# Gates of the weight sums through a table of their own, the sums spread over the stages, POOL left to their transfers

## The chip, the cores and the metric

One core of one Trainium2 chip runs the whole program in one launch. The metric is the device time of that launch in microseconds. Five engines are spoken of: PE (TensorE, the matmuls; PEld its weight loads), DVE (VectorE), ACT (ScalarE), POOL (GpSimd) and SP (SyncE, which here only issues transfers). POOL and SP both issue DMAs, POOL through the software queue, SP through the hardware queue.

## What is computed

A trunk of two layers on x of 1024 tokens and 1024 channels, with 256 memory tokens, all in float32. Cut to what matters:

```python
def reference(x, mem, ...):
    m = rms_norm(mem, mem_norm_g)
    h = x
    for layer in range(DEPTH):                      # DEPTH = 2
        hn = rms_norm(h, mix_norm_g[layer])
        if layer % 2 == 0:
            h = h + fourier_na_mixer(hn, w_in_ab[0], rpb[0], w_out_ab[0])
        else:
            h = h + short_gated_conv_mixer(hn, w_in_c[0], conv_c[0], w_out_c[0])
        h = h + memory_cross_attention(rms_norm(h, xa_norm_g[layer]), m, xa_wq[layer], xa_wkv[layer], xa_wo[layer])
        h = h + conv_ffn(rms_norm(h, ffn_norm_g[layer]), ffn_w_up[layer], ffn_conv_w[layer], ffn_conv_b[layer], ffn_w_down[layer])
    return rms_norm(h, final_norm_g)
```

The first mixer projects the 1024 channels to 2048: four Fourier groups of 128 channels (a 2-D FFT, real part) and q, k and v of four neighbourhood attention heads, whose scores get a bias `rpb` inside a window; both halves go through `w_out_ab`. The FFN has 2 x 2048 channels up, a width-3 convolution and a gelu gate, and 2048 back down.

## The kernel before

Every matmul is done as three passes over a number split in a high and a low part (`mm3`, L223 to L227: high x high at L225, high x low at L226, low x high at L227). A split (L218 to L221) is a cast on ACT (L220) for the high part and a subtraction (L221), on DVE or, where the caller says so, on POOL, for the low part. SBUF is a pool of 52 buffers of 128x1024 floats and four halves, all shown as `p`; a buffer is handed on as soon as its last reader is done, so an instruction that writes into it waits for that reader.

The stages follow one another: keys and values of the memory beside the first norm (to about 165 us), mixer 0 (to about 500), cross attention 0 (to about 725), a trunk of up0, down d0, convolution c and its output oc (to about 1515), cross attention 1 (to about 1775), and up1 with down d1 to the end. Inside a stage several generators run side by side (`run`, each with a cost as weight), and a scheduler fixes the order on each engine from them at build time.

Mixer 0 (L824 on) computes 16 blocks of the input projection (`proj_thread`): blocks 0 to 3 for the Fourier groups, 4 to 15 for q, k, v. `fft_thread` (memsets on POOL at L582, L583 and L640) and `na_thread` run beside it. `na_prep` loads for each head the mask (L750) and the bias (L752) by SP and subtracts one from the other on POOL (L753); the scores (L679, on DVE) add the table to what PE left in PSUM. `ahead` splits the four Fourier results, the odd ones on POOL. Then xT is loaded again (L499) and w_out is applied.

The FFNs, the convolution and oc are done by a scheme with seven products in place of eight for 2x2 blocks (Strassen and Winograd). Its weights come in 34 units (up0 8, d0 4, convolution 8, oc 2, up1 8, d1 4). Of each unit products 1, 2 and 4 read a quadrant of the weight, products 7, 6, 3 and 5 a sum of quadrants. These sums are made in DRAM by POOL's queue (`sums`, L1049 to L1063): four gates (L1059), each a DMA of one element from the tile that the caller has just written into the sum's own tile, which hold the copies back until the caller has got there; four copies of a quadrant (L1061); and four DMAs that add another one (L1063). Callers are the posts of the projection (L564, blocks 4 to 15), of the query projection (L883) and of the residual add (L816). `w_load` (L1066) reads a sum by SP when its product is near. `xb1` (L1115 on) starts an FFN: the norm's sum (matmul L328), the operands of the products, with ACT and DVE splits, up to the first result at DVE L1241. `put` (L1204) writes operands of the down projection to DRAM, `plan_down` (L1387) loads them back.

Of the kernel before, what the change touches and what calls it, by code (L numbers as in the profile page):

```python
# [47 lines left out]

CHAIN = {1: "a", 2: "a", 6: "b", 7: "b", 4: "b", 5: "c", 3: "c"}
OPENS, ENDS = (1, 6, 5), (2, 4, 3)  # L50
QUARTERS = ("11", "12", "21", "22")
COUPLES = (((0, 4), (1, 5)), ((2, 6), (3, 7)))


# [74 lines left out]
class Kern:  # L129
    def __init__(self, ctx, tc, ap):  # L130
        self.tc, self.nc, self.ap = tc, tc.nc, ap
        nc = self.nc
        sb = ctx.enter_context(tc.tile_pool(name="sb", bufs=1))
        ps = ctx.enter_context(tc.tile_pool(name="ps", bufs=1, space=bass.MemoryType.PSUM))
        dr = ctx.enter_context(tc.tile_pool(name="dr", bufs=1, space=bass.MemoryType.DRAM))
        self.sb = sb
        self.PSUM = ps.tile([P, 8 * 512], F32, name="PS")
        Pool.tick = 0
        self.pools = {2: Pool(NSLOT), 1: Pool(NHALF)}
        self.banks = Pool(8)  # L140
        self.kvd = [dr.tile([4, P, 2 * U], F32, name=f"kvd{i}") for i in range(2)]
        self.vec = sb.tile([P, NVEC], F32, name="vec")
        nc.sync.dma_start(self.vec, ap["vecs"])

        nc.vector.tensor_scalar(self.vec[:, 0:CONV_C], self.vec[:, 0:CONV_C], -1.0, None, op0=ALU.mult)
        self.ones = sb.tile([P, P], F32, name="ones")
        nc.vector.memset(self.ones, 1.0)
        self.ones_r = sb.tile([P, P], F32R, name="ones_r")
        nc.scalar.copy(self.ones_r, self.ones)
        self.ident = sb.tile([P, P], F32, name="ident")  # L150
        make_identity(nc, self.ident)
        self.eps = sb.tile([P, 1], F32, name="eps")
        nc.vector.memset(self.eps, EPS)
        warm = sb.tile([P, 1], F32, name="warm")
        nc.scalar.activation(warm, self.eps, AF.Abs_reciprocal_sqrt)
        self.small = sb.tile([P, 64], F32, name="small")
        self.nsmall = 0
        self.dr = dr
        self.q, self.did, self.op, self.xd, self.hd, self.wsrc = [], set(), {}, {}, {}, {}
        self.bg = None  # L160


    def sm(self, n):
# [363 lines left out]
    def proj_thread(self, blks, dst, head=0, tail=0, look=LOOK, hooks=()):  # L527

        nc = self.nc

        def psum(b, c):
            if b not in dst:
                dst[b] = [(yield from self.alloc(F32 if b < 4 or b >= 12 else F32R))]
                if 4 <= b < 12:
                    dst[b].append((yield from self.alloc(F32R)))
            self._b = yield from self.bank(1)
            self._bk[(b, c)] = self._b
            return self._b.f()

        self._bk = {}  # L540

        def post(b, c, ps):
            if b < 4:
                nc.scalar.copy(dst[b][0].f(c * CH, (c + 1) * CH), ps)
            else:

                def order(x):
                    return x.rearrange("p (s h r n) -> p s h r n", s=8, h=2, r=8)[:, :, c]
                i = ps.rearrange("p (r s n) -> p s r n", r=8, s=8)
                x = dst[b]  # L550
                if b < 8:
                    t = yield from self.alloc(F32, 1)
                    nc.scalar.activation(t.f(0, CH), ps, AF.Copy, scale=-(float(P) ** -0.5))
                    i = t.f(0, CH).rearrange("p (r s n) -> p s r n", r=8, s=8)
                if b < 12:
                    nc.scalar.copy(order(x[0].r()), i)
                    nc.vector.tensor_tensor(order(x[1].r()), i, order(x[0].f()), op=ALU.subtract)
                    if b < 8:
                        self.free(t)
                else:  # L560
                    nc.scalar.copy(order(x[0].f()), i)
            self.bfree(self._bk.pop((b, c)))
            self.done.add((b, c))
            if b >= 4 and c == 1:  # L564
                self.sums(dst[b][0].f(0, 1)[0:1])

        n = len(blks)
        o = [(blks[b], c) for b, c in self.order(n, min(head, n), tail)]
        yield from self.linear(o, self.ap["w_in"], KT, self.X_hn, psum, post, look=look, hooks=hooks)
# [4 lines left out]
    def fft_thread(self):  # L574
# [4 lines left out]
        nc.sync.dma_start(cs.f(0, 256), self.ap["dft_c"])  # L579
        Cm, Sm = cs.f(0, P), cs.f(P, 2 * P)  # L580
        alt = cs.f(256, 512)
        nc.gpsimd.memset(alt[:, ::2], 1.0)  # L582
        nc.gpsimd.memset(alt[:, 1::2], -1.0)  # L583
        tabs = yield from self.wload(self.ap["dft_s"], 4)
        H = 256

        for g in range(4):
# [49 lines left out]
            eo = yield from self.alloc(F32)  # L637
            y = self.yf[g] = yield from self.alloc(F32)
            nc.vector.scalar_tensor_tensor(e, alt, w[:, 3:4], be.f(0, H), op0=ALU.mult, op1=ALU.add)
            nc.gpsimd.memset(t.f(H, H + 1), 0.0)  # L640
            nc.scalar.copy(t.f(H + 1, 2 * H), bo.f(H + 1, 2 * H))

            nc.vector.scalar_tensor_tensor(y.f(H, H + 1), w[:, 4:5], w[:, 5:6], bo.f(H, H + 1),
# [101 lines left out]
    def na_prep(self, h):  # L745

        nc = self.nc
        hd = {"h": h, "p": {}, "pt": {}}
        m = yield from self.alloc(F32)
        nc.sync.dma_start(m.f(0, 896), self.ap["na_mask"])  # L750
        x = hd["tab"] = yield from self.alloc(F32)
        nc.sync.dma_start(x.f(0, 896), self.ap["na_bias"][h])  # L752
        nc.gpsimd.tensor_tensor(x.f(0, 896), m.f(0, 896), x.f(0, 896), op=ALU.subtract)  # L753
        self.free(m)
        while not self.ready(12 + h):
            yield None
        hd["q"], hd["k"], (x,) = (self.qkv[b + h] for b in (4, 8, 12))
        b = yield from self.bank(2)
        for j in range(8):
            nc.tensor.transpose(b.f(j * P, (j + 1) * P), x.f(j * P, (j + 1) * P), self.ident)  # L760
        hd["v"] = yield from self.wide_split(b.f())
        self.free(x)
        self.bfree(b)
        self.ya[h] = [(yield from self.alloc(F32R)), (yield from self.alloc(F32R))]
        yield 0.9
        return hd
# [34 lines left out]
    def res_post(self, st, fin=None):  # L801
# [8 lines left out]
        def post(b, c, ps):  # L810
# [3 lines left out]
            if st is not None:  # L814
                yield from self.sumsq(st, c, b, hc, CHUNKS[c][1])
                if b % 2 == 1:  # L816
                    self.sums(hc[0:1, 0:1])
            if fin is not None:
                yield from self.gained(fin, c, b)

# [1 line left out]

    def mixer0(self):
        nc = self.nc  # L824
        self.todo = self.up_items(0) + self.down_items("d0", 2, self.ap["w_down"][0])
        self.z, self.yf, self.qkv = {}, {}, {}
        self.done = set()
        self.run((self.proj_thread(range(0, 4), self.z, head=3), 42.0))
# [2 lines left out]
        def ahead():  # L831
            self.free_hn(0)
            for g in range(4):
                y = self.yf[g]
                self.yf[g] = yield from self.wide_split(y.f(), nc.gpsimd if g % 2 else nc.vector)
                self.free(y)

        def main():
# [21 lines left out]
    def xattn(self, l, st):  # L860
# [5 lines left out]
        def qproj(c, hooks=()):  # L866
# [6 lines left out]
            def post(b, cc, ps):  # L873
# [7 lines left out]
                self.bfree(bk.pop(b))  # L881
                qdone[c] = b
                if b % 2 == 1:  # L883
                    self.sums(lo.f(o, o + 1)[0:1])
            yield from self.linear([(b, c) for b in range(KT)], self.ap["wq"][l], KT, self.X_hn, psum, post,
                                   hooks=hooks)
            self.free_hn(c)
# [158 lines left out]
                n -= 1  # L1046


    def sums(self, gate):  # L1049


        if not self.todo:
            return
        key, src, n = self.todo.pop(0)
        g = self.nc.gpsimd
        d = {p: self.dr.tile([P, n], F32, name="ws_%s_%d" % ("_".join(map(str, key)), p)) for p in (7, 6, 3, 5)}
        self.wsrc[key] = {1: src[0], 2: src[1], 4: src[3], **d}
        for p in (7, 6, 3, 5):
            g.dma_start(d[p][0:1, 0:1], gate)  # L1059
        for p, i in ((7, 0), (5, 3), (6, 3), (3, 1)):  # L1060
            g.dma_start(d[p], src[i])  # L1061
        for p, more in ((7, src[2]), (5, src[2]), (6, d[7]), (3, d[6])):
            g.dma_start(d[p], more, accum_op=ALU.add, max_dma_last_dim=1024)  # L1063

    def w_load(self, key, p, n=2):
        def gen():  # L1066
# [134 lines left out]
    def put(self, tag, s, k, p, src):  # L1201

        o = (k % 2) * U
        self.nc.sync.dma_start(self.xd_tile(tag, s, p, k // 2)[:, o:o + U], src)  # L1204

    def put_rest(self, tag, s, k, a, b):

# [12 lines left out]
        self.put(tag, s, k, 5, t1)  # L1220
        self.put(tag, s, k, 3, b22)
        self.free(x, z, a, b)
        self.did.add((tag, "x", s, k))

    def opening(self, q, p, b, u, g, early):

# [160 lines left out]
    def plan_down(self, tag, segs):  # L1387
        def xload(s, p):
            for m in range(2):
                def gen(m=m):  # L1390
                    r = yield from self.alloc(F32)
                    self.nc.sync.dma_start(r.f(), self.xd[tag, s, p, m])
                    self.op.setdefault((tag, "X", s, p), []).append((yield from self.wide_split(r.f())))
                    self.free(r)
                self.task((tag, "X", s, p, m), 3, gen,
                          lambda: all((tag, "x", s, k) in self.did for k in range(4)))

        def row(k):
            def gen():
# [170 lines left out]
    def all(self):  # L1570
# [10 lines left out]
        self.plan_down("d0", 2)  # L1581
        self.plan_conv()
        self.plan_down("oc", 1)
        self.todo += [*self.conv_items(), *self.down_items("oc", 1, self.ap["w_out_c"]), *self.up_items(1)[:4]]
        st = self.xattn(0, st)
        st = self.trunk(st)
        self.plan_up(1)
        self.plan_down("d1", 2)
        self.todo += [*self.up_items(1)[4:], *self.down_items("d1", 2, self.ap["w_down"][1])]
        st = self.xattn(1, st)  # L1590
        self.last(st)

# [34 lines left out]

def _quads(w, pairs):


    return np.stack([np.concatenate([_quad(w, h, pr[e]) for pr in pairs], axis=1)
                     for e in range(2) for h in range(2)])


def _feat(v):
# [91 lines left out]
```

## Time and profile before

| | before |
|---|---|
| median of 3 runs | 2256.32 us (2249.65 to 2257.36) |
| profiled execution | 2262.05 us, span 2260.1, mean granted clock 0.979 |
| PE busy | 2172.6 us (96% of the span) |
| DVE busy | 1457.3 us (64%) |
| ACT busy | 946.1 us (42%) |
| POOL busy | 353.5 us (16%) |
| DMA, share of 16 engines' time | hardware queue 39.3%, software queue 27.4% |

Durations of single instructions and waits are from the one profiled execution. The busy time of an engine is a sum over the span; a PE that is busy at a granted clock under 1.00 does the same work in more time. A row of a timeline gives the start, the duration, the engine, the line, the operation, what is written and read, and in brackets how long the engine had been idle and what ended that. The DMA share counts 16 engines and can stand a little over 1.

### The profile page before, as it was taken

How to read it: one execution, taken by the hardware profiler on the slowest of the kernel's cores; microseconds unless marked ns; L12 is line 12 of the kernel's file. 1: busy time of each engine (PE TensorE's matmuls, PEld its weight loads, DVE VectorE, ACT ScalarE, POOL GpSimd, SP SyncE). 2: the span in 40 equal slices, each digit the busy share in tenths (PEclk: the TensorE clock that was granted, in tenths of full speed). 3: DMA queues.
4: the chain of work that ended last, by engine and by line, in shares of the span. 5: the costliest groups of instructions: out<-in, count | busy, mean ns of one | idle time of the engine just before them, and what ended most of it. 6: DMA issues, size and time to landing. Idle time of an engine off the chain costs nothing.

```text
span 2260.1 us, 26823 instructions
## 1 busy us (share of the span) xinstructions
PE 2172.6 (96%) x10174; PEld 1793.7 (79%) x10174; DVE 1457.3 (64%) x1989; ACT 946.1 (42%) x1362; POOL 353.5 (16%) x458
## 2 busy tenths in 40 slices
PE   9999886999999699999999999999999999999998
PEld 9988675888887577888888888888788778788887
DVE  6754334666656567758667667787566657766674
ACT  6532233344534433334544322345454533433553
POOL 5213444104332300000000000002431000000002
PEclk9999998999999799999999999999999999999999
DMA  9439999829999965538644234845998334456652
GB/s 370 145 101 223 231 240 280 194 85 274 249 244 279 282 148 177 176 109 314 239 154 168 75 121 143 283 160 186 281 282 228 131 117 138 148 175 236 257 177 75
DMA packets 177889, 446.10 MB, mean 197 GB/s; under 512 B 19808, under 2 KB 87648, under 8 KB 175584
## 3 DMA queue, kind: packets, MB, share of 16 engines
q1 hardware_dynamic: 101344, 310.14, 39.3%
q0 software_dynamic: 76416, 134.25, 27.4%
q8 instruction: 79, 1.29, 0.2%
q14 instruction: 50, 0.41, 0.1%
HBM read 386.64 MB, written 191.89 MB: 256 GB/s over the span
## 4 chain that ended last, share of the span: by engine, by line
PE 59%; DVE 3%; DMA 2%; ACT 1%; issue 0%; DVEq 0%; ACTq 0%; SPq 0%
PE PS L225 20%; PE PS L226 19%; PE PS L227 19%; DMA p<-in_wq_dram 1%; DVE p L221 1%; DMA p<-ws_u 1%; DMA xd_d<-p 1%; DVE p L1003 0%; ACT p L220 0%; DVE p L1005 0%; PE PS L929 0%; ACT p L1002 0%; DVE p L1295 0%; DVE p L1562 0%; PE PS L328 0%
## 5 line engine op out<-in xcount | busy, mean ns | idle before, releaser
L225 PE MATMUL PS<-p,p 128*128 128x512 f32 (+1 forms) x3264 | 1227.7, 381 | 67.0 <-ACT p L220 36.5
L226 PE MATMUL PS<-p,p 128*128 128x512 f32 (+1 forms) x3264 | 1236.1, 380 | 3.0 <-DVE p L221 3.0
L227 PE MATMUL PS<-p,p 128*128 128x512 f32 (+1 forms) x3264 | 1222.1, 378 | 3.1 <-DVE p L221 3.1
L220 ACT CAST p<-p 128x1024 fp32r<-128x1024 f32 (+1 forms) x566 | 528.8, 958 | 602.8 <-PE PS L226 111.0
L221 DVE TENSOR_TENSOR p<-p,p 128x1024 fp32r<-128x1024 f32 (+1 forms) x547 | 603.2, 1125 | 269.4 <-ACT p L220 199.4
L225 PEld LDWEIGHTS PS<-p,p 128*128 128x128 f32 x3264 | 619.3, 190 | 195.8 <-ACT p L220 41.8
L226 PEld LDWEIGHTS PS<-p,p 128*128 128x128 f32 x3264 | 619.5, 190 | 123.7 <-DVE p L221 4.9
L227 PEld LDWEIGHTS PS<-p,p 128*128 128x128 f32 x3264 | 617.8, 189 | 123.9 <-DVE p L221 4.2
L1059 POOL DMA_DIRECT2D ws_u<-p x64 | 37.7, 770 | 770.2 <-DVE p L879 748.3
L312 ACT ACTIVATE p<-p 128x512 f32<-128x512 f32 (+1 forms) x128 | 74.8, 590 | 125.1 <-DVE p L812 61.9
L318 DVE TENSOR_TENSOR p<-p,p 128x512 f32<-128x512 f32 (+1 forms) x111 | 80.0, 722 | 35.1 <-ACT p L312 32.9
L1562 POOL TENSOR_TENSOR p<-p,p 128x512 f32<-128x512 f32 (+1 forms) x15 | 16.4, 1128 | 504.4 <-DVE p L492 486.6
L220 ACT CAST p<-PS 128x512 fp32r<-128x512 f32 (+3 forms) x92 | 57.7, 633 | 81.0 <-PE PS L227 34.9
L221 DVE TENSOR_TENSOR p<-PS,p 128x512 fp32r<-128x512 f32 (+3 forms) x92 | 68.2, 745 | 33.0 <-ACT p L220 32.6
L812 DVE TENSOR_TENSOR p<-PS,p 128x512 f32<-128x512 f32 x64 | 44.1, 689 | 57.1 <-PE PS L227 57.0
L1002 ACT ACTIVATE p<-p,vec 128x1024 f32<-128x1024 f32 x32 | 39.7, 1241 | 67.0 <-DVE p L1287 54.3
L1003 DVE SCALAR_TENSOR_TENSOR p<-p,vec,p 128x1023 f32<-128x1023 f32 x40 | 51.2, 1280 | 18.8 <-ACT p L1002 18.4
L1283 DVE TENSOR_TENSOR p<-PS,p 128x512 f32<-128x512 f32 x32 | 22.1, 690 | 61.0 <-PE PS L227 61.0
L221 POOL TENSOR_TENSOR p<-p,p 128x1024 fp32r<-128x1024 f32 (+1 forms) x19 | 50.6, 2674 | 43.2 <-ACT p L220 42.8
L1005 DVE SCALAR_TENSOR_TENSOR p<-p,vec,p 128x1023 f32<-128x1023 f32 x40 | 51.1, 1278 | 0.4
L1063 POOL DMA_DIRECT2D ws_u<-ws_u x32 | 34.3, 1098 | 101.4 <-DMA ws_u<-in_w_up_dram 65.9
L1291 ACT ACTIVATE p<-p 128x1024 f32<-128x1024 f32 x32 | 33.9, 1060 | 36.5 <-DVE p L1005 36.5
(169 smaller groups left out, 1241.7 us busy)
## 6 DMA issues: line engine op xcount, KB each, us to landing
ws_u<-in_w_up_dram POOLq DMA_DIRECT2D x96, 512.0 KB, 9.1
p<-ws_u SPq DMA_DIRECT2D x64, 512.0 KB, 4.1
xd_d<-p SPq DMA_DIRECT2D x112, 256.0 KB, 5.1
p<-xd_d SPq DMA_DIRECT2D x56, 512.0 KB, 5.9
ws_d<-in_w_down_dram POOLq DMA_DIRECT2D x48, 512.0 KB, 13.4
p<-in_w_up_dram SPq DMA_DIRECT2D x48, 512.0 KB, 4.0
ws_u<-ws_u POOLq DMA_DIRECT2D x32, 512.0 KB, 9.4
p<-in_wq_dram SPq DMA_DIRECT2D x32, 512.0 KB, 4.2
```

Source lines behind the costliest of these rows:

```text
L220: self.nc.scalar.copy(hi, src)
L221: (eng or self.nc.vector).tensor_tensor(lo, src, hi.bitcast(F32), op=ALU.subtract)
L225: mm(ps, whi, xhi, start=first, stop=False, skip_group_check=True)
L226: mm(ps, whi, xlo, start=False, stop=False, skip_group_check=True)
L227: mm(ps, wlo, xhi, start=False, stop=last, skip_group_check=True)
L312: nc.scalar.activation(t.f(0, w), src, AF.Square)
L318: nc.vector.tensor_tensor(st[ch].f(0, w), st[ch].f(0, w), t.f(0, w), op=ALU.add)
L812: self.nc.vector.tensor_tensor(hc, ps, hc, op=ALU.add)
L1002: nc.scalar.activation(tmp.f(), src, AF.Identity, scale=v[:, w[1]:w[1] + 1], bias=v[:, bias:bias + 1])
L1003: nc.vector.scalar_tensor_tensor(tmp.f(1, S), src[:, 0:S - 1], v[:, w[0]:w[0] + 1], tmp.f(1, S), op0=ALU.mult, op1=ALU.add)
L1005: nc.vector.scalar_tensor_tensor(tmp.f(0, S - 1), src[:, 1:S], v[:, w[2]:w[2] + 1], tmp.f(0, S - 1), op0=ALU.mult, op1=ALU.add)
L1059: g.dma_start(d[p][0:1, 0:1], gate)
```

## The change

The program makes the following moves.

- **Gates.** `sums` gets a tile of 128x36 floats, `gates`. A copy on ACT takes a column of the caller's tile into the unit's own column of it, and the gates, two of them in place of four, read that column. Three of the sums of a unit (7, 6 and 3) now share one DRAM tile.
- **Order of a sum.** The quadrants are stored in another order, and the four sums are made one after the other, copy and addition: d0 = q0 + q3, d1 = q1 + d0, d5 = q1 + q3, d2 = q2 + d1. The third of them in the chain (d2) is added to the second, which is added to the first; the bytes are the same.
- **Spread.** In mixer 0 three of four posts with c = 1 make a sum, now from the Fourier blocks on, so 3 of the 12 units start there and 9 in blocks 4 to 15. Limits of 12, 26 and 34 units hold for the three stages that call `sums`.
- **POOL to DVE.** The memsets of the Fourier part, the subtraction of the attention table (L753, now L754) and the splits of the odd Fourier results.
- **Down projection.** An operand's load back waits for the two writes that it needs rather than for all writes of four rows.
- **Descriptor space** of the software queue: 2048 instead of 4096.

Among the instructions that wait for a transfer of POOL's queue, the order counts 23 on DVE and 25 on ACT before, none on either after the change; on SP 44 before and 114 after. SP's order ahead of the last head's bias and mask now holds three loads of xT where it held one.

```diff
             self.done.add((b, c))
-            if b >= 4 and c == 1:
-                self.sums(dst[b][0].f(0, 1)[0:1])
+            self.nposts = getattr(self, "nposts", -1) + (c == 1)
+            if c == 1 and self.nposts % 4 != 2:
+                self.sums(dst[b][0].f(0, 1))
...
-        nc.gpsimd.memset(alt[:, ::2], 1.0)
-        nc.gpsimd.memset(alt[:, 1::2], -1.0)
+        nc.vector.memset(alt[:, ::2], 1.0)
+        nc.vector.memset(alt[:, 1::2], -1.0)
...
-            nc.gpsimd.memset(t.f(H, H + 1), 0.0)
+            nc.vector.memset(t.f(H, H + 1), 0.0)
...
-        nc.gpsimd.tensor_tensor(x.f(0, 896), m.f(0, 896), x.f(0, 896), op=ALU.subtract)
+        nc.vector.tensor_tensor(x.f(0, 896), m.f(0, 896), x.f(0, 896), op=ALU.subtract)
...
-                    self.sums(hc[0:1, 0:1])
+                    self.sums(hc[:, 0:1])
...
-        self.todo = self.up_items(0) + self.down_items("d0", 2, self.ap["w_down"][0])
+        self.upto = 12
+        self.todo = [*self.up_items(0), *self.down_items("d0", 2, self.ap["w_down"][0]),
...
-                self.yf[g] = yield from self.wide_split(y.f(), nc.gpsimd if g % 2 else nc.vector)
+                self.yf[g] = yield from self.wide_split(y.f())
...
-    def sums(self, gate):
+    def sums(self, src):
...
-        if not self.todo:
+        if len(self.wsrc) >= self.upto:
             return
-        key, src, n = self.todo.pop(0)
+        key, q, n = self.todo.pop(0)
         g = self.nc.gpsimd
-        d = {p: self.dr.tile([P, n], F32, name="ws_%s_%d" % ("_".join(map(str, key)), p)) for p in (7, 6, 3, 5)}
-        self.wsrc[key] = {1: src[0], 2: src[1], 4: src[3], **d}
-        for p in (7, 6, 3, 5):
-            g.dma_start(d[p][0:1, 0:1], gate)
-        for p, i in ((7, 0), (5, 3), (6, 3), (3, 1)):
-            g.dma_start(d[p], src[i])
-        for p, more in ((7, src[2]), (5, src[2]), (6, d[7]), (3, d[6])):
-            g.dma_start(d[p], more, accum_op=ALU.add, max_dma_last_dim=1024)
+        i = len(self.wsrc)
+        gate = self.gates[:, i:i + 1]
+        self.nc.scalar.copy(gate, src)
+        name = "ws_" + "_".join(map(str, key))
+        d = self.dr.tile([3, P, n], F32, name=name)
+        d5 = self.dr.tile([P, n], F32, name=name + "_5")
+        self.wsrc[key] = {1: q[0], 4: q[1], 2: q[2], 7: d[0], 6: d[1], 3: d[2], 5: d5}
+        g.dma_start(d[:, 0:1, 0:1], gate[0:3])
+        g.dma_start(d5[0:1, 0:1], gate[0:1])
+        for to, x, more in ((d[0], q[0], q[3]), (d[1], q[1], d[0]), (d5, q[1], q[3]), (d[2], q[2], d[1])):
+            g.dma_start(to, x)
+            g.dma_start(to, more, accum_op=ALU.add, max_dma_last_dim=1024)
...
+        self.did.add((tag, "x", s, p, k))
...
-        self.did.add((tag, "x", s, k))
...
+                def ready(m=m):
+                    return all((tag, "x", s, p, 2 * m + e) in self.did for e in range(2))
+
...
-                self.task((tag, "X", s, p, m), 3, gen,
-                          lambda: all((tag, "x", s, k) in self.did for k in range(4)))
+                self.task((tag, "X", s, p, m), 3, gen, ready)
...
-                    dynamic_dma_scratch_size=4096)
+                    dynamic_dma_scratch_size=2048)
```

Where the order of instructions moves, at two places. The first is the attention table of head 2 in mixer 0. On POOL before, among gates, copies and additions of the sums (`ws_...` are the sums' tiles in DRAM, `p_...` buffers of SBUF; in brackets the semaphores waited for, DMASW those of POOL's transfers, DMAHW those of SP's):

```order
L1059 DMA ws_d_0_0_3_2809<-p_5_2713 1x1
L1059 DMA ws_d_0_0_5_2810<-p_5_2713 1x1 [waits DMASW1_49]
L1063 DMA ws_u_7_6_2692<-ws_u_7_7_2691 512x256 [waits DMASW4_49,DMASW2_49]
L753 TENSOR_TENSOR p_13_2871<-p_41_2869,p_13_2871 128x896 [waits DMAHW3_49,DMAHW5_49,DVE_49,PE_49]
L1061 DMA ws_d_0_0_7_2807<-in_w_down_dram 16x8192 [waits DMASW6_49,DMASW3_49]
L1061 DMA ws_d_0_0_5_2810<-in_w_down_dram 16x8192 [waits DMASW1_49]
```

And on DVE with the change:

```order
L684 RECIPROCAL small<-small 128x1 [waits Activation_49]
L685 TENSOR_SCALAR p_12_2106<-p_12_2106,small 128x384 [waits DVE_49]
L744 TENSOR_TENSOR p_36_2508<-PS,p_8_2507 128x2x16x8 [waits PE_49,Activation_49]
L754 TENSOR_TENSOR p_13_2858<-p_41_2856,p_13_2858 128x896 [waits DMAHW5_49,DMAHW3_49]
L680 ISA p_14_2107,small<-PS,p_1_2446 128x384 [waits PE_49]
L680 ISA small 128x1
```

The subtraction of this head's table has gone from behind an addition of the sums on POOL to a place among the scores of the head before it (L680, L679 in the kernel before) on DVE, where it waits for two loads of SP.

The second place is ACT at the start of up0, before:

```order
L220 CAST p_27_6217<-p_19_6057 128x1024 [waits DVE_49]
L1236 COPY p_47_6095<-PS 128x512 [waits PE_49]
L220 CAST p_44_6159<-p_18_5679 128x1024 [waits DMASW4_49,DMASW3_49,DMASW5_49,DMASW2_49,DMASW6_49,DMASW1_49,DMASW7_49,DMASW0_49,DVE_49]
L220 CAST p_3_6163<-p_26_5686 128x1024 [waits DMASW7_49,DMASW1_49,DMAHW3_49,DMASW0_49,DVE_49]
L1236 COPY p_48_6109<-PS 128x512 [waits PE_49]
```

and with the change:

```order
L220 CAST p_27_6140<-p_19_5980 128x1024 [waits DVE_49]
L1246 COPY p_47_6018<-PS 128x512 [waits PE_49]
L220 CAST p_44_6082<-p_18_5608 128x1024 [waits DVE_49]
L220 CAST p_3_6086<-p_26_5615 128x1024 [waits DMAHW3_49,DVE_49]
L1246 COPY p_48_6032<-PS 128x512 [waits PE_49]
```

The order is the same; the waits of two casts on POOL's transfers are not there any more.

## Rows read from the trace of the kernel before

**Rows 1.** Stretches: us, then busy time (instructions) of PE, PEld, DVE, ACT, POOL; PEclk, DMA share, GB/s.

```profile
120.00:165.00 45.00, 45.00 (x214) 37.31 (x213) 22.63 (x44) 15.06 (x26) 4.81 (x12) 1.00 0.27 96
...
240.00:420.00 180.00, 143.55 (x674) 119.57 (x673) 75.90 (x177) 60.87 (x133) 72.70 (x98) 0.90 1.07 255
...
1400.00:1440.00 40.00, 40.00 (x175) 32.55 (x174) 29.53 (x39) 9.71 (x12) 0.00 (x0) 1.00 0.62 205
```

**Rows 2.** Timeline of PE where it stood still in mixer 0.

```profile
271.32 0.80 PE L225 MATMUL PS<-p,p 128*128 128x512 f32 x1 [7.55 <-DVE small L679]
...
332.19 0.69 PE L225 MATMUL PS<-p,p 128*128 128x384 f32 x1 [6.64 <-ACT p L220]
...
378.87 0.69 PE L225 MATMUL PS<-p,p 128*128 128x384 f32 x1 [14.49 <-DVE small L679]
```

**Rows 3.** Timeline of DVE at the same three places.

```profile
269.70 1.22 DVE L221 TENSOR_TENSOR p<-p,p 128x1024 fp32r<-128x1024 f32 x1 [17.94 <-DMA ws_u<-p]
...
332.09 0.42 DVE L679 CUSTOM_DVE_ANT_0 p<-PS,p 128x256 f32<-128x256 f32 x1 [14.53 <-POOL p L753]
...
378.38 0.42 DVE L679 CUSTOM_DVE_ANT_0 p<-PS,p 128x256 f32<-128x256 f32 x1 [14.38 <-POOL p L753]
```

**Rows 4.** Timeline of POOL at head 2's table.

```profile
328.90 1.06 POOL L1063 DMA_DIRECT2D ws_u<-ws_u  x1 [6.57 <-DMA ws_u<-in_w_up_dram]
329.60 2.46 POOL L753 TENSOR_TENSOR p<-p,p 128x896 f32<-128x896 f32 x1
```

**Rows 5.** Timeline of SP's queue: loads of mask (L750) and bias (L752).

```profile
277.26 0.33 SPq L750 DMA_DIRECT2D p<-in_na_mask_dram  x1
...
297.92 0.33 SPq L752 DMA_DIRECT2D p<-in_na_bias_dram  x1
...
342.92 0.65 SPq L750 DMA_DIRECT2D p<-in_na_mask_dram  x1
```

**Rows 6.** DMA issues, 275 to 310 us: form and count, KB each, median us to landing.

```profile
p<-in_na_bias_dram SPq DMA_DIRECT2D x1, 448.0 KB, 9.1
ws_u<-p POOLq DMA_DIRECT2D x8, 0.0 KB, 12.5
```

**Rows 7.** Timelines at the start of up0 (727 on) and of up1 (1775 on).

```profile
727.43 1.02 PE L328 MATMUL PS<-p,ones 128*128 128x512 f32 x2
...
752.56 1.99 ACT L220 CAST p<-p 128x1024 fp32r<-128x1024 f32 x2 [12.64 <-DMA ws_u<-p]
...
790.35 0.69 DVE L1241 TENSOR_TENSOR p<-PS,p 128x512 f32<-128x512 f32 x1 [0.25 <-PE PS L227]
...
1775.80 1.02 PE L328 MATMUL PS<-p,ones 128*128 128x512 f32 x2
...
1820.60 0.69 DVE L1241 TENSOR_TENSOR p<-PS,p 128x512 f32<-128x512 f32 x1 [0.26 <-PE PS L227]
```

**Rows 8.** Stretches behind the three waits, columns as in Rows 1.

```profile
271.00:281.00 10.00, 9.16 (x26) 7.09 (x27) 6.82 (x18) 4.32 (x10) 5.36 (x8) 0.59 1.08 287
332.00:338.00 6.00, 5.04 (x14) 4.13 (x15) 5.53 (x14) 5.52 (x11) 4.04 (x7) 0.56 1.21 359
379.00:390.00 11.00, 8.91 (x33) 7.40 (x34) 7.42 (x21) 5.21 (x14) 3.00 (x5) 0.73 1.11 323
```

**Rows 9.** DMA issues, 340 to 346 us.

```profile
p<-in_na_mask_dram SPq DMA_DIRECT2D x1, 448.0 KB, 10.8
```

**Rows 10.** DMA issues, 727 to 790 us.

```profile
p<-ws_u SPq DMA_DIRECT2D x7, 512.0 KB, 6.7
```

**Rows 11.** DMA issues, 1776 to 1821 us.

```profile
p<-ws_u SPq DMA_DIRECT2D x7, 512.0 KB, 3.2
```

**Rows 12.** Groups of instructions: busy us, mean ns of one, idle time ahead and what ended it.

```profile
L221 DVE TENSOR_TENSOR p<-p,p 128x1024 fp32r<-128x1024 f32 (+1 forms) x547 | 603.2, 1125 | 269.4 <-ACT p L220 199.4 <-PE PS L226 29.5 <-DMA ws_u<-p 27.4
...
L155 ACT ACTIVATE warm<-eps 128x1 f32<-128x1 f32 x1 | 0.2, 203 | 0.0
```

**Rows 13.** DMA issues, 0 to 170 us.

```profile
ws_u<-p POOLq DMA_DIRECT2D x4, 0.0 KB, 1.6
```

More of the change, by code (lines that the diff above doesn't have):

```diff
@@ L50 @@
 OPENS, ENDS = (1, 6, 5), (2, 4, 3)
-QUARTERS = ("11", "12", "21", "22")
 COUPLES = (((0, 4), (1, 5)), ((2, 6), (3, 7)))
@@ L160, in __init__ @@
         self.bg = None
+        self.gates = sb.tile([P, 36], F32, name="gates")
     def sm(self, n):
@@ L824, in mixer0 @@
         nc = self.nc
-        self.todo = self.up_items(0) + self.down_items("d0", 2, self.ap["w_down"][0])
+        self.upto = 12
+        self.todo = [*self.up_items(0), *self.down_items("d0", 2, self.ap["w_down"][0]),
+                     *(((n,), self.ap["w_cc" if n[0] == "c" else "w_cb"][int(n[1])], 2 * U if n[0] == "c" else U)
+                       for n in sorted(self.CONV_SEQ, reverse=True, key=lambda n: (n[0], -int(n[1])))),
+                     *self.down_items("oc", 1, self.ap["w_out_c"]), *self.up_items(1),
+                     *self.down_items("d1", 2, self.ap["w_down"][1])]
         self.z, self.yf, self.qkv = {}, {}, {}
@@ L883, in post @@
                 if b % 2 == 1:
-                    self.sums(lo.f(o, o + 1)[0:1])
+                    self.sums(lo.f(o, o + 1))
             yield from self.linear([(b, c) for b in range(KT)], self.ap["wq"][l], KT, self.X_hn, psum, post,
@@ L1583, in all @@
         self.plan_down("oc", 1)
-        self.todo += [*self.conv_items(), *self.down_items("oc", 1, self.ap["w_out_c"]), *self.up_items(1)[:4]]
+        self.upto = 26
         st = self.xattn(0, st)
@@ L1588, in all @@
         self.plan_down("d1", 2)
-        self.todo += [*self.up_items(1)[4:], *self.down_items("d1", 2, self.ap["w_down"][1])]
+        self.upto = 34
         st = self.xattn(1, st)
@@ L1631, in _quads @@
     return np.stack([np.concatenate([_quad(w, h, pr[e]) for pr in pairs], axis=1)
-                     for e in range(2) for h in range(2)])
+                     for e, h in ((0, 0), (1, 1), (0, 1), (1, 0))])
 def _feat(v):
```

## The prediction

> **What bounds it now.** I read the table of stretches first. In an undisturbed stretch TensorE is busy for all of 40 us at a clock of 1.00, while VectorE has a quarter of its time free; from 240 to 420 us it is busy for 143.55 of 180 us, at 0.90, and the DMA engines are full (1.07) [rows 1]. TensorE is the bound, then, and what a change can win is its idle time and the slow clock behind it. Next I read its timeline where it stands still: 7.55, 6.64 and 14.49 us, behind VectorE and ScalarE [rows 2]. VectorE's own timeline tells why. Ahead of 269.70 it waited 17.94 us for `ws_u<-p`, a gate: four bytes read out of a buffer that the next split was to overwrite. Twice it waited over 14 us for POOL's L753, the attention table [rows 3]. POOL's timeline shows that L753 was not slow but late: it stood behind L1063, which had waited 6.57 us for a weight copy to land before it could issue [rows 4]. VectorE got to its wait at 332.09 - 14.53 = 317.56, when the bias (issued 297.92, 9.1 to land) had been there since 307.0 [rows 3, 5, 6].
>
> The second place is the start of the first FFN. Its twin in the last layer runs the same chain, from the norm's first matmul L328 to the first L1241, with no sums beside it: 1820.60 - 1775.80 = 44.80 us. The first takes 790.35 - 727.43 = 62.92, with ScalarE at L220 waiting 12.64 us for a gate [rows 7]. The difference is 18.1.
>
> **The change, part by part.** The sum is made against the profiled execution, 2262.05 us (span 2260.1), which lies 5.7 above the median of 2256.32; I take what it gives off the median.
>
> *Waits in the mixer.* The gates read a table that nothing overwrites, and the subtraction leaves POOL, so both kinds of wait lose their cause. Idle: 7.55 + 6.64 + 14.49 = 28.7 [rows 2]. The clock stayed low after each: 0.59 over 9.16 busy us costs 9.16 x 0.41 = 3.8, then 5.04 x 0.44 = 2.2 and 8.91 x 0.27 = 2.4 [rows 8], in all 8.4. Together 37.1.
>
> *What is late next there.* VectorE now waits for mask and bias itself, at the place of the subtraction, and its softmax steps are queued behind. Head 2 has 317.56 - 307.0 = 10.5 us in hand. Head 3: VectorE came at 378.38 - 14.38 = 364.0, the mask had landed at 342.92 + 10.8 = 353.7, so 10.3 [rows 3, 5, 9]. With the stalls gone VectorE comes 7.55 + 3.8 = 11.4 earlier to head 2 and 20.2 earlier to head 3. If the loads came no earlier, head 2 would wait 0.9, head 3 9, and the two xT loads that SP now issues ahead of head 3's table add 1 MB at 255 GB/s [rows 1], 4.1: about 15 with some clock. If the loads move up with the buffers that they wait for, nothing. I take the middle, **8 put back (0 to 15)**.
>
> *Start of the first FFN.* ScalarE's and VectorE's waits for gates go: up to 18.1. But the sums still run there, and a weight load takes 6.7 us instead of the twin's 3.2 [rows 10, 11]. One load late is 3.5, two in turn 7; I take **5 put back (0 to 7)**.
>
> *What is added.* VectorE gets four subtractions of 896 columns, by L221 1125 x 896/1024 = 0.98 each, 3.9; two of 1024 (the yf splits), 2.3; six memsets of at most 256 columns, under 0.28 each, 1.7. ScalarE gets 34 copies of one column at 0.20, 6.9 [rows 12]. Of these 14.8 us most lie in idle time, VectorE being busy for 75.90 of 180 us there [rows 1]; where TensorE waits for a split the cover is gone. **Plus 3 (0 to 7)**, half of it as the upper end.
>
> *What I cost at nothing.* The sums' new order has one accumulation more in its chain (0, then 1, then 3) and two gates instead of four, for the same bytes, and POOL may wait longer at the head of its queue; no compute is left behind it there, and the sums have long been there when they are read. Three of them start in the Fourier blocks, where the DMA share is 0.27 [rows 1], which can only thin the crowd behind. Half the descriptor space could hold POOL up; I bound that by the slack too, 0 to 4, and take 0, because it delays sums and no engine. The finer readiness of the down projection's loads meets a TensorE that is busy 40.00 of 40 us [rows 1]: nothing to win.
>
> The sum: -37.1 + 8 - 18.1 + 5 + 3 = -39.2, that is **2217**. With every put-back at its low end it is -55.2, 2201; with all at the high end (15 + 7 + 7) it is -26, 2230.
>
> *A rule against it.* The gates themselves took 12.5 us to land (median) between 275 and 310 us, and 1.6 before 170, when the DMA engines were a quarter busy [rows 1, 6, 13]. The Trainium skill (DMA: Bandwidth & Descriptors, section Anatomy of one DMA — SWDGE (gpsimd) path) gives a DMA from this queue a fixed cost of about 2.0 us plus its bytes at 436 GB/s. By that rule a gate lands in 2 us and cannot hold a buffer for long, and the time is that of the rival in which the gates were not the cause. The trace agrees before 170 us and differs sixfold later, so the measured landing decides.
>
> **The rivals.** *The loads take over.* The DMA engines stay full, and what waited for a gate waits for its data. For: share 1.07, tables landing in 9.1 and 10.8 where the twin's loads take 3.2 [rows 1, 6, 9, 11]. Five loads lie on the path (tables of two heads, the first of w_out, two weights of the FFN); each late by 9.1 - 3.2 = 5.9, 30 comes back in place of 13: -22, **2234**. Against: VectorE found the tables landed 10 us before. The Trainium skill (same page, section Issuing engines are not separate DMA queues) says that transfers from all queues run on the same 16 engines and interleave; the bias's 9.1 beside full engines agrees, and by that rule this rival is the outcome.
>
> *The gates were not the cause.* The wait at 269.70 named several sources, and the last may have been a load; then only POOL's two stalls go: 6.64 + 14.49 + 2.2 + 2.4 = 25.7, less 8 and 3, -15, **2242**. Against: 12.5 to land fits a wait of 17.94 and one of 12.64 [rows 3, 6, 7].
>
> *It does not do what it says.* All gates share one table; were it followed as a whole, each copy into a column would wait for the gates before it, and ScalarE would stand where VectorE stood: **2256**. Against: in the order of instructions ScalarE's and VectorE's 48 waits on POOL's transfers are 0 after the change; what speaks for it is only that other waits may fill the place.
>
> *Slower.* VectorE works in order. POOL could wait for the bias without harm; VectorE cannot. In head 2 the bias was issued 20.66 us after the mask [rows 5] and took 9.1 to land. If VectorE reaches the subtraction when the mask is issued, it stands 29.8 us; TensorE has 14.53 - 6.64 = 7.9 in hand, so 21.9 and 3 of clock, 25 a head; three heads 75, against 55.2 - 3 won: +23, **2279**. It decides from 52.2 / 3 = 17 a head. Against: the subtraction stands right ahead of the scores that need it, where the trace shows the table landed.
>
> **How the numbers follow.** Forecast 0.58, loads 0.20, gates not the cause 0.07, no effect 0.08, slower 0.07. A measurement here can tell about 0.5%, 11 us, from no change: under 2245 counts as faster, over 2267.6 as slower. The first three cases are faster, 0.85. The range runs from 2199, just past the low ends, to 2242, which takes in the loads' case and touches the gates' case.
>
> **What would show it.** Right: VectorE's waits for POOL's table and both engines' waits for `ws` gates are gone; TensorE's clock is at 1.00 over most of 240 to 420; from L328 to L1241 about 50 us in the first FFN; POOL computes only in the memory's keys and values and in the final norm. Wrong: a new wait of VectorE at L754 for the bias of over 10 us a head, TensorE waiting behind splits whose load lands late, or L328 to L1241 still near 60.

## The result, and the profile after

The changed kernel takes **2218.64 us** (median of 4 runs, 2215.65 to 2226.15) where the kernel before, run beside it, takes 2252.99 (2248.17 to 2257.36): a ratio of **0.9853, interval 0.9816 to 0.9890**. The forecast was 2217, within 2199 to 2242; it was a gain of 39.2 us from 2256.32, and 34.4 are measured. The profiled execution has a span of 2224.2 against 2260.1.

The line of the page with each engine's busy us, share of the span and instructions:

```profile
PE 2163.2 (97%) x10174; PEld 1787.2 (80%) x10174; DVE 1459.4 (66%) x2001; ACT 947.8 (43%) x1396; POOL 304.5 (14%) x378
```

The stretches that answer to [rows 1], and two of the first FFN (columns as there):

```profile
120.00:165.00 45.00, 45.00 (x213) 37.32 (x213) 23.14 (x48) 14.77 (x28) 9.58 (x14) 1.00 0.79 201
...
240.00:420.00 180.00, 177.46 (x859) 148.92 (x858) 97.21 (x210) 68.81 (x149) 38.12 (x54) 0.99 0.82 203
...
760.00:800.00 40.00, 29.45 (x120) 23.27 (x119) 21.41 (x26) 11.99 (x12) 9.17 (x14) 0.87 0.87 227
...
840.00:880.00 40.00, 31.17 (x124) 24.88 (x123) 25.70 (x32) 12.46 (x13) 8.24 (x12) 0.87 1.00 292
```

In the mixer TensorE is now busy for 177.46 of 180 us, where it was 143.55, at a clock of 0.99. The DMA share there is 0.82, where it was 1.07, and 0.79 in the Fourier blocks, where it was 0.27. But from 760 to 880 us TensorE stands still again. The timelines of VectorE at the tables and at the first result of up0, and of TensorE:

```profile
291.32 1.09 DVE L754 TENSOR_TENSOR p<-p,p 128x896 f32<-128x896 f32 x1 [7.45 <-DMA p<-in_na_bias_dram]
...
329.72 1.09 DVE L754 TENSOR_TENSOR p<-p,p 128x896 f32<-128x896 f32 x1 [4.62 <-DMA p<-in_na_mask_dram]
...
733.67 0.69 DVE L1251 TENSOR_TENSOR p<-PS,p 128x512 f32<-128x512 f32 x1 [0.25 <-PE PS L227]
```

```profile
685.43 1.02 PE L328 MATMUL PS<-p,ones 128*128 128x512 f32 x2
...
780.00 0.80 PE L225 MATMUL PS<-p,p 128*128 128x512 f32 x1 [10.55 <-ACT p L220]
...
853.04 0.80 PE L225 MATMUL PS<-p,p 128*128 128x512 f32 x1 [8.83 <-ACT p L220]
```

VectorE does wait for the tables' data, 7.45 and 4.62 us, and TensorE has no stall for it. From L328 to the first L1251 the first FFN takes 733.67 - 685.43 = 48.24 us, where L328 to L1241 took 62.92 [rows 7]. Then two new stalls come, 10.55 and 8.83 us. ScalarE, in the same places:

```profile
778.90 1.04 ACT L220 CAST p<-p 128x1024 fp32r<-128x1024 f32 x1 [10.68 <-DMA xd_d<-p]
...
851.95 1.04 ACT L220 CAST p<-p 128x1024 fp32r<-128x1024 f32 x1 [9.62 <-DMA p<-ws_u]
```

It waits for an operand's write to leave its buffer, and for a weight to land. The DMA issues from 800 to 855 us (count, KB each, median us to landing):

```profile
xd_d<-p SPq DMA_DIRECT2D x14, 256.0 KB, 12.4
...
p<-ws_u SPq DMA_DIRECT2D x6, 512.0 KB, 9.0
```

and before the change in the stretch with the same work, 848 to 903 us:

```profile
p<-ws_u SPq DMA_DIRECT2D x8, 512.0 KB, 4.2
xd_d<-p SPq DMA_DIRECT2D x14, 256.0 KB, 4.8
```

What makes them slow is the sums, which still run there. POOL's last addition of the second stage, before and after:

```profile
803.97 1.03 POOL L1063 DMA_DIRECT2D ws_u<-ws_u  x1 [6.79 <-DMA ws_u<-ws_u]
```

```profile
943.90 1.03 POOL L1073 DMA_DIRECT2D ws_u<-ws_u  x1 [5.25 <-DMA ws_u<-ws_u]
```

The waits view of the changed kernel (us in total, times, longest) says what held them up; before, the same wait stood at 38.4 us for `ws_d` and 8.1 for `ws_u`:

```profile
POOL ws_u L1073 <- issue: 324.4, 46, 17.5
...
POOL ws_d L1073 <- issue: 150.1, 22, 11.3
...
POOL ws_c L1073 <- issue: 92.6, 13, 12.2
```

"issue" is time in which the engine waited for nothing that the profile shows.

Both kernels have 10174 matmuls in almost the same order. How much earlier the n-th one starts after the change, in the two profiled executions; a step is what the stretch up to that row adds to the time, with a minus where it is shorter:

```
n-th matmul, time before            earlier by    step
2100    409.5  mixer, past its stalls  43.6       -43.6
3620    733.2  end of cross attention  42.0        +1.6
3800    797.6  start of up0            56.7       -14.7
4300    919.4  rest of up0             34.4       +22.3
6600   1452.4  d0 and convolution      33.5        +0.9
6900   1522.3  oc                      29.1        +4.4
7300   1612.4  into cross attention 1  35.0        -5.9
10173  2250.9  rest of it, up1, d1     36.2        -1.2
```

One profile is not exact to a few us here: e9 below has the same code in up0 and loses 16.4 there, not 22.3.

### The profile page after: what moved, and what is told of

Its sections match the earlier page's. It is cut to its first block, busy times and chain, and to the rows that moved or that the text cites. A ratio compares the mean times of both kernels' runs of the same rounds, so it can differ in the third digit from the quotient of the medians.

```text
span 2224.2 us, 26698 instructions
## 1 busy us (share of the span) xinstructions
PE 2163.2 (97%) x10174; PEld 1787.2 (80%) x10174; DVE 1459.4 (66%) x2001; ACT 947.8 (43%) x1396; POOL 304.5 (14%) x378
## 4 chain that ended last, share of the span: by engine, by line
PE 85%; DVE 6%; DMA 6%; ACT 1%; issue 1%; SPq 0%; POOL 0%; DVEq 0%; ACTq 0%; POOLq 0%
PE PS L225 28%; PE PS L226 28%; PE PS L227 27%; DVE p L221 2%; DMA p<-ws_u 2%; DMA xd_d<-p 1%; DMA p<-in_wo_dram 1%; ACT p L220 1%; PE PS L935 1%; DVE p L1009 1%; DMA p<-in_na_mask_dram 1%; DVE p L1011 0%; DVE p L1109 0%; DMA p<-in_w_in_dram 0%; PE PS L328 0%
## 5 line engine op out<-in xcount | busy, mean ns | idle before, releaser
L225 PE MATMUL PS<-p,p 128*128 128x512 f32 (+1 forms) x3264 | 1221.5, 380 | 38.7 <-ACT p L220 35.5
L226 PE MATMUL PS<-p,p 128*128 128x512 f32 (+2 forms) x3264 | 1232.9, 379 | 6.5 <-DVE p L221 6.3
L227 PE MATMUL PS<-p,p 128*128 128x512 f32 (+1 forms) x3264 | 1219.1, 377 | 0.9 <-DVE p L221 0.7
L1069 POOL DMA_DIRECT2D ws_u<-gates x16 | 13.5, 841 | 608.4 <-ACT gates L1064 608.4
L1574 POOL TENSOR_TENSOR p<-p,p 128x512 f32<-128x512 f32 (+1 forms) x15 | 16.4, 1123 | 408.9 <-DVE p L492 391.2
L1073 POOL DMA_DIRECT2D ws_u<-in_w_up_dram x32 | 33.5, 1046 | 237.0 <-issue 186.5
L221 POOL TENSOR_TENSOR p<-p,p 128x1024 fp32r<-128x1024 f32 (+1 forms) x17 | 45.3, 2677 | 43.1 <-ACT p L220 42.7
```

The source lines that it names most:

```text
L221: (eng or self.nc.vector).tensor_tensor(lo, src, hi.bitcast(F32), op=ALU.subtract)
L225: mm(ps, whi, xhi, start=first, stop=False, skip_group_check=True)
L226: mm(ps, whi, xlo, start=False, stop=False, skip_group_check=True)
L227: mm(ps, wlo, xhi, start=False, stop=last, skip_group_check=True)
L1073: g.dma_start(to, more, accum_op=ALU.add, max_dma_last_dim=1024)
```

## The experiments

Theory A, formed on these rows: the halved descriptor space holds POOL up at its additions, and the late sums fall on the first FFN's transfers. Rival B: the sums are late because of their order and place. Four runs take one part each.

**e1, the space.** To make room for the 4096 bytes the table has 8 columns, used in turn.

```diff
-        self.gates = sb.tile([P, 36], F32, name="gates")
+        self.gates = sb.tile([P, 8], F32, name="gates")
...
-        i = len(self.wsrc)
+        i = len(self.wsrc) % 8
...
-                    dynamic_dma_scratch_size=2048)
+                    dynamic_dma_scratch_size=4096)
```

> The changed kernel with the descriptor space back at 4096; to make room the gates' table has 8 columns used in turn. Theory A (the halved space holds POOL up at its additions, so the second stage's sums end at 938 us instead of 804 and fall on the first FFN's loads): POOL's waits named issue fall from 567 us to under 100, the sums of the second stage end near 800, TensorE's two stalls of 10.55 and 8.83 us in the first FFN go, and the time falls by about 20 to 2195 to 2205; the mixer may give back up to 8 of this through fuller DMA engines. Rival B (the sums are late because each unit is one chain and starts in another place): the space changes nothing, 2213 to 2224, the sums still end near 930.

Measured 0.9822 (0.9795 to 0.9848), 2217.7 us, as the changed kernel. The mechanism is A's: POOL's "issue" waits at `ws_u` fall from 324.4 to 34.2, the sums end at 785, and the rest of up0 loses 2.5 us in place of 22.3. The forecast of 2195 to 2205 is a miss, since in its profile 7.6 are lost again in the mixer and 4.6 at the start of up0: the DMA share from 240 to 420 us is 0.94 in place of 0.82, and ScalarE waits for loads. That the fuller engines cause this is not shown: e7 below has a share of 1.10, and from 360 to 395 us TensorE has no stall. ScalarE's timeline in e1:

```profile
362.98 1.04 ACT L220 CAST p<-p 128x1024 fp32r<-128x1024 f32 x1 [10.29 <-DMA p<-in_w_out_dram]
...
730.28 1.04 ACT L220 CAST p<-p 128x1024 fp32r<-128x1024 f32 x1 [7.62 <-DMA p<-ws_u]
```

**e2, the space alone**, in the kernel before.

```diff
-                    dynamic_dma_scratch_size=4096)
+                    dynamic_dma_scratch_size=2048)
```

> The kernel before with the descriptor space halved and nothing else. Theory A: POOL's waits named issue rise from under 100 to several hundred us, the sums of the second stage end 80 us or more later than 804, and since POOL still holds the attention tables, which then stand behind more waiting, the time rises to 2260 to 2285. Rival B: no effect, 2248 to 2258, sums end near 804.

Measured **1.0674** (1.0657 to 1.0691), 2408.54 us: A's direction, but a loss of 152 us where 29 was its upper end. Its waits view:

```profile
POOL ws_u L1063 <- issue: 278.1, 49, 12.1
POOL ws_d L1063 <- issue: 177.6, 29, 12.6
...
DVE p L679 <- POOL p L753: 81.6, 2, 41.5
...
ACT p L220 <- DMA ws_u<-p: 57.6, 1, 57.6
```

The table and the gates stand in POOL's queue behind the held additions, and VectorE and ScalarE behind them. Alone, this part of the change would cost 152 us.

**e3, gates on the callers' tiles.**

```diff
-        gate = self.gates[:, i:i + 1]
-        self.nc.scalar.copy(gate, src)
+        gate = src
```

> The changed kernel, gates reading the callers' tiles again (two gates a unit, no copies on ScalarE). If the gates held buffers: waits of VectorE and ScalarE for gates are back, the mixer loses up to 7.55 + 3.8 = 11 us and the start of the first FFN up to 15, 2228 to 2245. If the waits put down to gates were another's: 2214 to 2222, as the changed kernel or a little faster for the 34 copies saved.

Measured 1.0746 (1.0717 to 1.0774), 2426.26 us: the waits for gates are back, as the first case said, but the time is 181 us over its range, a miss in size. VectorE now waits 84.0 us for one gate:

```profile
DVE p L221 <- DMA ws_u<-p: 94.5, 2, 84.0
```

**e4, the work back on POOL** (tables, odd Fourier splits, memsets): the diff ahead of the prediction, the other way round for these lines.

```diff
-        nc.vector.tensor_tensor(x.f(0, 896), m.f(0, 896), x.f(0, 896), op=ALU.subtract)
+        nc.gpsimd.tensor_tensor(x.f(0, 896), m.f(0, 896), x.f(0, 896), op=ALU.subtract)
```

> The changed kernel with the attention tables' subtraction, the odd Fourier splits and the memsets back on POOL. If POOL's place in the queue was the cause: VectorE waits for POOL's table again, at least the 6.64 + 14.49 + 4.6 = 25.7 us of before come back, more since POOL now waits at its additions: 2240 to 2275. If only the gates mattered: 2214 to 2224.

Measured 1.0411 (1.0378 to 1.0444), 2346.86 us, the first case's direction and 72 us over its range; VectorE waits 89.7 us in all for the table:

```profile
DVE p L680 <- POOL p L754: 89.7, 3, 32.2
```

With the halved space each of the two parts is worth far more than the stalls of the kernel before, because each keeps the other engines out of a queue that has become slower. What they are worth at the old space, the next two show.

**e5 and e6, one part each in the kernel before.**

```diff
+        i = len(self.wsrc) % 8
+        col = self.gates[:, i:i + 1]
+        self.nc.scalar.copy(col, gate)
+        gate = col[0:1]
```

> The kernel before with one part of the change: gates read a table (8 columns in turn, a copy on ScalarE each); POOL keeps its subtractions, the space stays 4096, the four gates and the order of the sums as before. By the sum: the gates' stall of 7.55 + 3.8 us in the mixer and most of the 14.7 won at the start of the first FFN go, POOL's two stalls (25.7) stay: 25 less, 2225 to 2238. If the two kinds of wait hide each other (a gate's wait taken away only brings the table's wait sooner): 2240 to 2252.

```diff
-        nc.gpsimd.tensor_tensor(x.f(0, 896), m.f(0, 896), x.f(0, 896), op=ALU.subtract)
+        nc.vector.tensor_tensor(x.f(0, 896), m.f(0, 896), x.f(0, 896), op=ALU.subtract)
...
-                self.yf[g] = yield from self.wide_split(y.f(), nc.gpsimd if g % 2 else nc.vector)
+                self.yf[g] = yield from self.wide_split(y.f())
```

> The kernel before with the other part alone: tables, odd Fourier splits and memsets on VectorE, gates on the callers' tiles, space 4096. By the sum: the 25.7 us of POOL's stalls go and the gates' stalls stay: 2225 to 2240. If the two hide each other, the gates' waits at the same places (13.0 us of ScalarE beside the second stall) take over: 2238 to 2252.

The gates alone give 0.9951 (0.9936 to 0.9967), the work moved 0.9941 (0.9916 to 0.9965): 11 and 13 us, in both cases about half of what the sum says. (The kernel before took 2250.46 us beside them, 6 less than the 2256 from which the ranges start; so the gains are compared, not the times of 2238.18 and 2237.34.) At the 2100th matmul e5 is 5.7 us ahead and e6 15.1, where the terms of their parts give 11.4 and 25.7. In e5 the second wait for POOL's table grows from 14.53 [rows 3] to 22.14, and the stall of TensorE there from 6.64 [rows 2] to 17.59:

```profile
327.23 0.42 DVE L680 CUSTOM_DVE_ANT_0 p<-PS,p 128x256 f32<-128x256 f32 x1 [22.14 <-POOL p L754]
...
328.79 0.69 PE L227 MATMUL PS<-p,p 128*128 128x384 f32 x1 [17.59 <-DVE p L222]
```

and in e6 VectorE and ScalarE stand at gates, where they waited 17.94 and 13.0 us before, and at a third place, where there was no wait for a gate:

```profile
265.97 1.22 DVE L221 TENSOR_TENSOR p<-p,p 128x1024 fp32r<-128x1024 f32 x1 [16.72 <-DMA ws_u<-p]
...
328.12 0.48 ACT L220 CAST p<-PS 128x384 fp32r<-128x384 f32 x1 [14.39 <-DMA ws_d<-p]
...
384.19 1.04 ACT L220 CAST p<-p 128x1024 fp32r<-128x1024 f32 x1 [11.68 <-DMA ws_d<-p]
```

The two kinds of wait hide each other: with one gone, the other lasts longer (e5) or shows up where the first one stood (the third place in e6).

**e10, both parts together**, nothing else of the change.

> The kernel before with both the gates' table and the work moved to VectorE, and nothing else (four gates a unit, old order of the sums, space 4096, no spread, old readiness). If the two parts hide each other's gain, the mixer is 40 us shorter here, against 5.8 and 15.1 for each alone, and the time is that of e7 less the 4 us of the readiness: 2207 to 2217. If the new order of the sums and the two gates fewer are needed for it: 2222 to 2236.

Measured **0.9801** (0.9782 to 0.9821), 2209.56 us, as the first case said. At the 2100th matmul it is 42.0 us ahead, twice 5.7 + 15.1 (5 of them are lost again by 500 us). From 240 to 420 us:

```profile
240.00:420.00 180.00, 174.17 (x848) 145.55 (x847) 90.94 (x200) 66.85 (x148) 61.29 (x90) 1.00 1.04 258
```

The order of the sums, two gates fewer, the spread and the smaller space are not needed for the gain.

**e7 and e12, without the spread**, at 4096 (as e1) and at 2048.

```diff
-            if c == 1 and self.nposts % 4 != 2:
+            if c == 1 and b >= 4:
```

> The changed kernel with space 4096 (table of 8 columns, as e1) and the first 12 sums where they were, in blocks 4 to 15. If the spread matters only through the crowd in the mixer: DMA share of 240 to 420 back near 1.05, the load of w_out that held ScalarE 10.29 us in e1 lands no earlier, sums end later than 785, 2216 to 2230. If the spread is worth nothing: 2212 to 2220 as e1.

> The changed kernel (space 2048) without the spread. If the spread is what keeps the halved space harmless (it starts the sums 13 us earlier, with 3 units done in the Fourier blocks): the second stage's sums end 30 us or more after 938 and the first FFN loses more than 22: 2224 to 2240. If it is worth nothing at this space either: 2213 to 2224.

At 4096 the spread gives nothing: 0.9835 (0.9817 to 0.9854) without it, 0.9822 with. The crowd forecast for e7 came, and cost nothing, as its stretch from 240 to 420 us shows:

```profile
240.00:420.00 180.00, 176.12 (x851) 147.32 (x850) 90.30 (x200) 66.97 (x147) 59.04 (x82) 0.99 1.10 277
```

At 2048 it is 0.9889 (0.9868 to 0.9911) without, 2228.08 us, and 0.9853 with; the sums end at 970, not 944. The median is where the first expectation put it, but the intervals overlap, so whether the spread helps at this space stays unclear. What the space does without the spread is clear: e12 and e7 differ in it (and in the columns of the table), and their intervals are apart. The halved space costs 0.5% there, some 12 us; by the profiles the rest of up0 loses 17.6 us in e12 and 6.1 in e7, and d0 with the convolution 5.1 and none.

**e8, eight of the sums in the trunk**, in the changed kernel.

```diff
-        self.upto = 26
+        self.upto = 22
         st = self.xattn(0, st)
+        self.upto = 30
...
             yield from self.sumsq(st2, c, k, self.hch(k, c), CHUNKS[c][1])
+            if tag == "d0" and c == 1:
+                self.sums(self.hch(k, c)[:, 0:1])
```

> The changed kernel with 4 of the second stage's 14 sums and 4 of the third stage's 8 made in the trunk, at the end of d0, where the DMA share is 0.22 to 0.43; space 2048. Theory A (late sums on top of the first FFN's loads cost 22 us): the second stage's sums end near 830, at least one of the two stalls of 10.55 and 8.83 us goes, and the stall of 5.31 us in the third stage shrinks: 2195 to 2210. If those stalls come from the FFN's own loads and writes, whoever else is there: 2214 to 2224.

Measured 0.9894 (0.9867 to 0.9921), 2225.49 us, above both ranges. The sums of the second stage end at 786, and the rest of up0 loses 1.3 us in place of 22.3: with e1, where they end early for another reason, this shows that the late sums were the cause. But the convolution and oc, which now run beside sums, lose 10.7 and 7.2, and the later part of cross attention 1 another 5.0. One of the stretches, where the changed kernel has a DMA share of 0.43 and TensorE busy throughout:

```profile
1240.00:1300.00 60.00, 56.90 (x240) 45.77 (x239) 37.52 (x49) 15.70 (x20) 8.97 (x12) 0.97 0.98 288
```

**e9, the old readiness** of the down projection's loads.

```diff
-                    return all((tag, "x", s, p, 2 * m + e) in self.did for e in range(2))
+                    return all((tag, "x", s, p, k) in self.did for k in range(4) for p in range(1, 8))
```

> The changed kernel with the down projection's loads waiting for all writes again. If the finer readiness brought the loads of oc forward and with them splits that crowd VectorE (10.00 of 10 us busy at 1455) ahead of the convolution's own: the stall of 2.60 us at 1455 goes, the stretch from the convolution to oc is 4 us shorter, 2212 to 2217. If the readiness gains elsewhere what it loses there (as I costed it at nothing): 2217 to 2222.

The step at oc is 0.5 us, where it was 4.4, so the place is right; the other profiles agree, with 4.4 to 7.2 in all that have the finer readiness (e1, e3, e4, e7, e8, e12 and the change itself) and at most 0.5 in all that have the old one (e2, e5, e6, e10, e11). The time is 0.9856 (0.9829 to 0.9883), no different from 0.9853; in its profile 7.4 us more go in the later part of cross attention 1 instead. What the finer readiness is worth in all, this run can't tell. The crowd is plain in the changed kernel, VectorE busy for 10.00 of 10 us:

```profile
1455.00:1465.00 10.00, 7.41 (x33) 6.00 (x33) 10.00 (x13) 1.22 (x2) 0.00 (x0) 1.00 0.32 105
```

**e11, a version to beat both:** e7 with the old readiness and

```diff
-        self.upto = 26
+        self.upto = 24
```

> A version meant to beat both: table of 8 columns, space 4096, no spread, old readiness, and 2 of the second stage's 14 sums left to the third stage. Second stage's sums end near 750, so the stall of 8.61 us of e7 in the first FFN goes, and with the old readiness 4 more: 2195 to 2205. If the stall comes from the FFN's own loads: 2208 to 2214.

Measured **0.9787** (0.9765 to 0.9808), 2205.84 us, below the changed kernel's interval. The sums end at 734. The rest of up0 is now free, but TensorE stalls for 12.39 us at its start, behind ScalarE's wait of 9.67 us for a weight:

```profile
721.72 1.04 ACT L220 CAST p<-p 128x1024 fp32r<-128x1024 f32 x1 [9.67 <-DMA p<-ws_u]
...
722.82 0.80 PE L225 MATMUL PS<-p,p 128*128 128x512 f32 x1 [12.39 <-ACT p L220]
```

```profile
760.00:800.00 40.00, 37.53 (x162) 29.85 (x161) 30.82 (x37) 16.00 (x17) 0.00 (x0) 1.00 0.42 140
```

so the time falls between the two cases. The gain over e10, 0.9801, lies within the intervals.

## Why the prediction was right

The main mechanism was right. That the time came so close is in part luck: terms that were off in opposite directions nearly cancel.

- *Waits in the mixer, 37.1.* Measured 43.6, with the other small stalls of that stretch. Shown by e10 (42.0 for the two parts alone). The sum added their stalls as if each were to be had for itself; e5 and e6 show that they are not. One of the small stalls is the moved work's too: in the kernel before TensorE stands 2.19 us behind a scaling on VectorE that takes 3.80 us beside one of POOL's splits, where the next of the same form takes 0.42. With the splits on VectorE all 32 of these scalings take at most 0.42.

```profile
359.21 3.80 DVE L684 TENSOR_SCALAR p<-p,small 128x384 f32<-128x384 f32 x1
...
360.02 2.77 POOL L221 TENSOR_TENSOR p<-p,p 128x1024 fp32r<-128x1024 f32 x1
...
363.07 0.96 PE L694 MATMUL PS<-ident,p 128*128 128x128 f32 x5 [2.19 <-DVE p L684]
```

- *Put back, 8.* Measured none: VectorE waits 7.45 and 4.62 us at L754, and TensorE stands for no more than 0.45 us beside them. Both waits are under the 7.9 us that TensorE had in hand before; that this is the reason is argued, not shown. The rival "the loads take over" falls in the mixer, where e7 has a DMA share of 1.10 and TensorE 176.12 busy of 180 us; in the rest of up0 loads that land late did take over. The slower rival falls by the waits at L754, both far under 17.
- *Start of the first FFN, 13.* Measured 14.7, and 14.4 in e5 from the gates alone. The rival in which the gates were not the cause falls. With it falls, here, the rule of the Trainium skill (DMA: Bandwidth & Descriptors, section Anatomy of one DMA — SWDGE (gpsimd) path) that such a transfer costs about 2.0 us and its bytes: four bytes took 12.5 [rows 6], and VectorE and ScalarE waited 17.94 and 12.64 us for buffers that such gates read [rows 3, 7].
- *What was added, 3.* A subtraction takes 1.09 us, where 0.98 was worked out. No separate cost of it can be seen; no run took it alone.
- *Costed at nothing: the step that failed.* "It delays sums and no engine", 0 to 4, was wrong. The halved space delayed the sums by 140 us, into the first FFN's transfers, whose weights then took 9.0 us instead of 4.2, and 22.3 us went there (16.4 in e9's profile of the same code), against 2.5 in e1 and 1.3 in e8, where the sums end early. The Trainium skill (same page, section Issuing engines are not separate DMA queues) says that transfers of all queues share the same 16 engines; the rows agree, with those 9.0 and 4.2. The finer readiness, also costed at nothing, shows 4.4 at oc (e9). The new order of the sums does not lengthen their chain, as the forecast has it: 7, 6 and 3 hung on one another before, too. What is new in it is that the copies stand between the additions.

So -43.6 + 1.6 - 14.7 + 22.3 + 0.9 + 4.4 - 5.9 - 1.2 give -36.2, where the sum said -39.2. The mixer came out 17.5 better than forecast (43.6 for 37.1 - 8 - 3), and 26.7 went in the rest of up0 and in oc, which the forecast had at nothing. The 5.9 won going into cross attention 1 are in no term of it either: a stall of 3.79 us at 1599.6, behind a load of that stage's weights, is gone, and no run was made to show why.

That POOL waits for room for its descriptors at "issue" is the reading of e1 and e2, in which the space changes (and in e1 the columns of the table); the profile does not name what it waits for.

## What to carry to other kernels

A transfer that reads a working buffer holds that buffer until it is done, and in a full queue that can be long (84.0 us in e3); so let gates read a place that nothing else needs, and keep other engines' work out of a queue that waits for data. Stalls that share a queue hide each other: take them out together before judging either. And when transfers are only delayed, look at which stage they will fall into; "off the critical path" holds for a place, not for a stream that can slide 140 us.

## What was not expected of the hardware

Halving the software queue's descriptor space raised POOL's waits at the additions of the kernel before from 46.5 us to 455.7 at `ws_u` and `ws_d`, and the kernel's time by 6.7% (e2). In the changed kernel, where no engine's work stands behind those additions, the same step costs far less: 0.9853 against 0.9822 with the spread, within the intervals (e1), and 0.9889 against 0.9835 without it, some 12 us and outside them (e12 against e7). It keeps the DMA share of the mixer at 0.82, where e1 has 0.94 and e7 1.10. By the profiles of the changed kernel and e1 it loses 19.8 us in the rest of up0 and wins 12.2 of them in the mixer and at the start of up0.
